# An ordering edge behind each score's relu for the projection work between the indexer's scores of row blocks 2 and 3

## The chip, the cores and the metric

The kernel runs on one core of a Trainium2 chip. The metric is the device time of one execution in microseconds (us). Engines are named as in the profile: PE (matrix products, with PEld for its weight loads), ACT, DVE, POOL, and SP, which here only issues DMAs. Every engine works through its own queue in order; engines wait for each other through semaphores. A line number L374 is a line of the kernel before; in the kernel after, lines from 365 on stand one or two further down.

## The reference

One transformer block over 512 positions of width 1024, in float32. Branch A is sparse attention: an indexer scores all pairs, each row keeps its best 128 keys, and a softmax with a relative bias runs over those. Branch B is stick-breaking attention. Gates, an output projection, a layer norm and a gated MLP with a causal convolution follow.

```python
proj = x @ w_in[layer]
q_a, k_a, v_a, q_i, k_i, w_i, q_s, k_s, v_s, g_a, g_b = jnp.split(proj, IN_OFFSETS, axis=-1)
...
dots = jnp.einsum('thd,sd->ths', qib, k_idx).astype(jnp.float32) * IDX_DIM ** -0.5
score = jnp.einsum('th,ths->ts', wib.astype(jnp.float32), jax.nn.relu(dots))
score = jnp.where(key_chunk[None, :] <= q_chunk, score, -jnp.inf)
_, sel = lax.top_k(score, n_sel)
...
log_beta = jax.nn.log_sigmoid(z)
log_keep = jnp.where(causal, jax.nn.log_sigmoid(-z), 0.0)
later = lax.cumsum(log_keep, axis=2, reverse=True) - log_keep
a = jnp.where(causal, jnp.exp(log_beta + later), 0.0).astype(v.dtype)
```

## The kernel before

Every float32 operand is split into a high part and the remainder (names ending in h and l, or whi and wlo for weights), and a product is made of three matmuls: high by high, high by low, low by high. A weight piece is loaded by SP, its high part is made by ACT (L101) and its low part by DVE or, for the projections in POOL_LO (qs, ks, gb, qa0, ka0, va), by POOL (L103). The pieces run through rings of three buffers, three loads and three splits ahead of use (`Stream`), so a split waits for the last matmul on the piece three before it.

**The projections are fillers.** FILL lists them in order: the rest of the value projection vs, then query, key and gate projections (qs0, ks0, ..., gb, qa, ka, va). `fill(n)` issues the next n matmuls of that list, and at a projection's end its evictions: the copy on ACT (L252 for values, L326 for queries, L315 and L316 for keys), the remainder on DVE (L253, L327, L317, L318), for queries also a DMA from ACT's queue (L328). The fillers fill the gaps of the attention work: three matmuls after each score, GAP = 15 at three points of each head.

**The scores.** `idx_scores` (L365) runs over row blocks j = 1, 2, 3 and eight heads: two matmuls into a bank of pool psA (`dot_ps`, L371, L372; 256, 384, 512 columns for the three blocks), a relu on ACT into an SBUF tile (L374), and a multiply-add on DVE into score j (L377, L379). psA has four banks, shared with the projections of the fillers. At each step of the loop (L580) one selection round is issued for j > 1, and then `fill(3)`.

**Selection.** `select` finds the best 128 of each row in 16 rounds of MAX and MATCH_REPLACE on DVE (L388, L389) and ends with a TENSOR_SCALAR (L391). The rounds left over are spread over the heads by ROUNDS.

**Heads.** Eight stick-breaking heads, then eight sparse ones. For each the next head's logits are issued first (z_ps, L452, with two sigmoids on ACT, L456 and L457), then the weights of this one are transposed (tr_ps, L410; evicted to pth on ACT, L414, and ptl on DVE, L415), then the next head's running products are made by four scans on DVE (L466) and a product on POOL (beta, L468), then the value product (av_ps, L426, with avt on ACT, L431, and yst on DVE, L432). A sparse head has logits l_ps (L490) with a reduction (L494) on DVE, an exponential on ACT (L496) and a scaling on DVE (L502), and a mask bm on POOL (L479).

**What sets the order.** The code's order is not the final one: a scheduler reorders the instructions of every engine by a simulated timeline, within the dependencies. `tc.issue_after(x)` adds one: whatever is issued inside it stays behind instruction x in the order. The kernel uses it at L602 to L605 for scans and selection.

## Time and profile before

| | us |
|---|---|
| median of 3 runs | 762.83 (762.15 to 762.95) |
| profiled execution, its own time | 762.16 |
| its span, first to last instruction | 760.4 |
| PE busy | 748.6 |
| DVE busy | 555.4 |
| ACT busy | 379.3 |
| POOL busy | 153.5 |
| granted clock of TensorE | 0.998 |

The page gives the busy time of each engine, the chain of work that ended last, and the costliest groups. The waits view lists, for each engine, the instruction that waited, what released it, the total, the count and the longest. The timeline lists instructions of one engine by start and duration; like neighbours are drawn together with a count, and square brackets give the idle time before an instruction and what ended it. In the timeline the durations of PE overlap, since matmuls are pipelined; what a matmul costs is the distance between starts.

The scores run from about 49 to 66 us, the heads follow, then the output projection and the MLP. The stretches that matter below are the scores and the heads from 150 to 212 us, which include the end of the stick-breaking heads and the first sparse ones.

### The profile page before, as it was taken

How to read it: one execution, taken by the hardware profiler on the slowest of the kernel's cores; microseconds unless marked ns; L12 is line 12 of the kernel's file. 1: busy time of each engine (PE TensorE's matmuls, PEld its weight loads, DVE VectorE, ACT ScalarE, POOL GpSimd, SP SyncE). 2: the span in 40 equal slices, each digit the busy share in tenths (PEclk: the TensorE clock that was granted, in tenths of full speed). 3: DMA queues.
4: the chain of work that ended last, by engine and by line, in shares of the span. 5: the costliest groups of instructions: out<-in, count | busy, mean ns of one | idle time of the engine just before them, and what ended most of it. 6: DMA issues, size and time to landing. Idle time of an engine off the chain costs nothing.

```text
span 760.4 us, 9842 instructions
## 1 busy us (share of the span) xinstructions
PE 748.6 (98%) x3573; PEld 627.3 (82%) x3573; DVE 555.4 (73%) x905; ACT 379.3 (50%) x568; POOL 153.5 (20%) x160
## 2 busy tenths in 40 slices
PE   9999999999999999999999999999999999999995
PEld 7878888887888888888889888888888888888885
DVE  5569787799878585548765867766776768668995
ACT  5474756655574756835364633433443344346430
POOL 1002555426644210000111110111011101110012
PEclk9999999999999999999999999999999999999999
DMA  8445433232223324116942344544444444448632
GB/s 267 147 128 181 125 95 96 72 111 84 80 102 111 111 76 122 64 60 206 340 61 84 139 156 136 155 137 139 153 140 142 147 138 137 141 152 274 222 105 79
DMA packets 40448, 102.89 MB, mean 135 GB/s; under 512 B 10888, under 2 KB 11272, under 8 KB 40400
## 3 DMA queue, kind: packets, MB, share of 16 engines
q1 hardware_dynamic: 34672, 85.98, 35.4%
q0 software_dynamic: 3728, 11.04, 4.0%
q10 hardware_dynamic: 2000, 5.24, 2.8%
q8 instruction: 28, 0.46, 0.3%
q14 instruction: 20, 0.16, 0.1%
HBM read 88.59 MB, written 9.98 MB: 130 GB/s over the span
## 4 chain that ended last, share of the span: by engine, by line
PE 92%; DVE 5%; issue 1%; ACT 0%; POOL 0%; POOLq 0%; ACTq 0%; DVEq 0%
PE u_ps L774 5%; PE u_ps L776 5%; PE g_ps L774 5%; PE u_ps L775 5%; PE g_ps L776 5%; PE g_ps L775 5%; PE m L856 2%; PE m L854 2%; PE m L855 2%; PE av_ps L426 2%; PE ga_ps L224 2%; PE ga_ps L223 2%; PE ga_ps L225 2%; PE o_ps L704 2%; PE o_ps L703 2%; PE o_ps L705 2%
## 5 line engine op out<-in xcount | busy, mean ns | idle before, releaser
L101 ACT ACTIVATE whi<-raw 128x1024 fp32r<-128x1024 f32 (+1 forms) x124 | 124.1, 1001 | 169.5 <-PE g_ps L775 44.9
L103 DVE TENSOR_TENSOR wlo<-raw,whi 128x1024 fp32r<-128x1024 f32 (+1 forms) x105 | 120.0, 1144 | 41.3 <-ACT whi L101 40.5
L776 PE MATMUL u_ps<-x1h,wlo 128*128 128x512 f32 (+1 forms) x192 | 71.4, 372 | 0.0
L774 PE MATMUL u_ps<-x1h,whi 128*128 128x512 f32 (+1 forms) x192 | 71.3, 372 | 0.0
L775 PE MATMUL u_ps<-x1l,whi 128*128 128x512 f32 (+1 forms) x192 | 71.3, 371 | 0.0
L774 PE MATMUL g_ps<-x1h,whi 128*128 128x512 f32 (+1 forms) x184 | 69.9, 380 | 0.0
L775 PE MATMUL g_ps<-x1l,whi 128*128 128x512 f32 (+1 forms) x184 | 69.9, 380 | 0.0
L776 PE MATMUL g_ps<-x1h,wlo 128*128 128x512 f32 (+1 forms) x184 | 69.9, 380 | 0.0
L103 POOL TENSOR_TENSOR wlo<-raw,whi 128x1024 fp32r<-128x1024 f32 x19 | 45.8, 2412 | 34.5 <-ACT whi L101 34.4
L776 PEld LDWEIGHTS u_ps<-x1h,wlo 128*128 128x128 f32 x192 | 36.2, 188 | 6.3
L775 PEld LDWEIGHTS u_ps<-x1l,whi 128*128 128x128 f32 x192 | 36.2, 188 | 6.3
L774 PEld LDWEIGHTS u_ps<-x1h,whi 128*128 128x128 f32 x192 | 36.2, 188 | 6.2
L415 DVE TENSOR_TENSOR ptl<-tr_ps,pth 128x512 fp32r<-128x512 f32 (+1 forms) x48 | 27.9, 595 | 18.2 <-ACT pth L414 17.6
L776 PEld LDWEIGHTS g_ps<-x1h,wlo 128*128 128x128 f32 x184 | 34.6, 188 | 6.6
L775 PEld LDWEIGHTS g_ps<-x1l,whi 128*128 128x128 f32 x184 | 34.6, 188 | 6.5
L774 PEld LDWEIGHTS g_ps<-x1h,whi 128*128 128x128 f32 x184 | 34.6, 188 | 6.5
L797 DVE TENSOR_TENSOR t<-raw 128x512 f32<-128x512 f32 x11 | 7.6, 693 | 40.2 <-DMA raw<-in_w_fo_dram 40.2
L816 POOL MEMSET u<- 128x2 f32 x22 | 2.1, 98 | 143.7 <-ACT whi L101 99.9
L830 DVE TENSOR_TENSOR hF<-g_ps,c 128x512 f32<-128x512 f32 x22 | 15.1, 687 | 20.4 <-PE g_ps L776 20.4
L822 ACT ACTIVATE c<-c,cwt 128x512 f32<-128x512 f32 x22 | 16.0, 725 | 26.3 <-DVE c L821 26.1
L672 POOL TENSOR_TENSOR rstd<-rstd,mhalf 128x1 f32<-128x1 f32 x8 | 7.6, 951 | 106.0 <-DVE rstd L671 106.0
L414 ACT ACTIVATE pth<-tr_ps 128x512 fp32r<-128x512 f32 (+1 forms) x48 | 23.9, 520 | 9.8 <-PE tr_ps L410 6.8
(566 smaller groups left out, 2055.9 us busy)
## 6 DMA issues: line engine op xcount, KB each, us to landing
raw<-in_w_fi_dram SPq DMA_DIRECT2D x44, 512.0 KB, 3.3
raw<-in_w_t_dram SPq DMA_DIRECT2D x32, 512.0 KB, 3.4
raw<-in_w_fo_dram SPq DMA_DIRECT2D x26, 512.0 KB, 4.2
raw<-in_w_br_dram SPq DMA_DIRECT2D x8, 512.0 KB, 3.3
raw<-in_w_o_dram SPq DMA_DIRECT2D x8, 512.0 KB, 4.2
raw<-in_w_v_dram SPq DMA_DIRECT2D x7, 512.0 KB, 3.9
raw_b<-in_w_fo_dram SPq DMA_DIRECT2D x6, 512.0 KB, 4.2
s_t<-t POOLq DMA_DIRECT2D x11, 256.0 KB, 2.3
```

What stands on the lines that cost most here:

```text
L101: nc.scalar.activation(hi[:, :w], t[:, :w], AF.Copy)
L103: self.done[key] = eng.tensor_sub(lo[:, :w], t[:, :w], r32(hi[:, :w])).ins
L223: nc.tensor.matmul(ps[:M], wh[:, c], xh[k], start=(k == 0), stop=False)
L224: nc.tensor.matmul(ps[:M], wh[:, c], xl[k], start=False, stop=False)
L225: nc.tensor.matmul(ps[:M], wl[:, c], xh[k], start=False, stop=(k == KC - 1))
L414: nc.scalar.activation(th[:, :width], ps[:, :width], AF.Copy)
L415: lows = nc.vector.tensor_sub(tl[:, :width], ps[:, :width], r32(th[:, :width]))
L426: nc.tensor.matmul(ps[:, 128 * i:512], vt[i][:, h].rearrange("p a d -> p (a d)"), t[i], start=(n == 0), stop=(n == len(seq) - 1))
L774: nc.tensor.matmul(ps[:, c], wh[:, kc], x1h[:, k, c], start=(k == 0), stop=False)
L775: nc.tensor.matmul(ps[:, c], wh[:, kc], x1l[:, k, c], start=False, stop=False)
L776: nc.tensor.matmul(ps[:, c], wl[:, kc], x1h[:, k, c], start=False, stop=(k == KC - 1))
L822: nc.scalar.activation(c, c, AF.Gelu_apprx_tanh, bias=cwt[:, f, 3:4])
```

## The change

`idx_scores` hands out, with j, the relu instruction of the score before. For the steps of j > 1, that is from block 2's first score on, the loop issues `fill(3)` inside `issue_after` of that relu: whatever a filler issues there on ScalarE, split or eviction, is ordered behind the last score's relu. No computation is added or taken away, and no operand changes.

```diff
--- before.py
+++ after.py
@@ -362,16 +362,17 @@
 
     def idx_scores():
         kih, kil, wi = index["k"]
+        last = None
         for j in (1, 2, 3):
             N = 128 * (j + 1)
             for h in range(H):
-                yield j
+                yield j, last
                 ps = pa("dot_ps")
                 r = slice(j * 128, j * 128 + 128)
                 nc.tensor.matmul(ps[:, :N], qi[h][:, r], kih[:, :N], start=True, stop=False)
                 nc.tensor.matmul(ps[:, :N], qi[h][:, r], kil[:, :N], start=False, stop=True)
                 rl = bp.tile([128, 512], F32, tag="pt", bufs=8, name="relu")
-                nc.scalar.activation(rl[:, :N], ps[:, :N], AF.Relu, scale=0.125)
+                last = nc.scalar.activation(rl[:, :N], ps[:, :N], AF.Relu, scale=0.125).ins
                 w = wi[:, j - 1, h:h + 1]
                 if h == 0:
                     nc.vector.tensor_scalar(score[j], rl[:, :N], w, None, op0=ALU.mult)
@@ -577,10 +578,11 @@
     nc.gpsimd.dma_start(s_win, bass.AP(tensor=s_line.tensor, offset=s_line.offset + 127,
                                        ap=[[NREL, H], [-1, 128], [1, 512]]))
 
-    for j in idx_scores():
+    for j, last in idx_scores():
         if j > 1:
             select_some(1)
-        fill(3)
+        with tc.issue_after(last) if j > 1 else nullcontext():
+            fill(3)
     heads = [("s", h) for h in range(H)] + [("a", h) for h in range(H)]
 
     def start_head(i):
```

The edge changes the scheduler's timeline, so it also moves rows far behind the scores, through the heads. Three places follow. At the first, ACT in the middle of the scores, relu_478 to relu_547 are block 1's, those with 384 columns block 2's; vs0 to vs3 are the evictions of the value projection, whi_16 is a split for a weight piece. Before:

```order
L374 ACTIVATE relu_478<-dot_ps_475 128x256
L252 ACTIVATE vs0_704<-vs_ps0_163 128x8x64
L252 ACTIVATE vs1_707<-vs_ps1_164 128x8x64
L374 ACTIVATE relu_487<-dot_ps_484 128x256
L252 ACTIVATE vs2_710<-vs_ps2_165 128x8x64
L374 ACTIVATE relu_496<-dot_ps_493 128x256
L374 ACTIVATE relu_505<-dot_ps_502 128x256
L101 ACTIVATE whi_16_604<-raw_16_602 128x1024
L252 ACTIVATE vs3_713<-vs_ps3_166 128x8x64
L374 ACTIVATE relu_520<-dot_ps_517 128x256
L374 ACTIVATE relu_529<-dot_ps_526 128x256
```

After, from the fourth relu of block 1 on:

```order
L375 ACTIVATE relu_505<-dot_ps_502 128x256
L375 ACTIVATE relu_520<-dot_ps_517 128x256
L375 ACTIVATE relu_529<-dot_ps_526 128x256
L375 ACTIVATE relu_538<-dot_ps_535 128x256
L375 ACTIVATE relu_547<-dot_ps_544 128x256
L375 ACTIVATE relu_560<-dot_ps_557 128x384
L375 ACTIVATE relu_572<-dot_ps_569 128x384
L375 ACTIVATE relu_584<-dot_ps_581 128x384
L375 ACTIVATE relu_596<-dot_ps_593 128x384
L101 ACTIVATE whi_16_604<-raw_16_602 128x1024
L375 ACTIVATE relu_614<-dot_ps_611 128x384
L375 ACTIVATE relu_626<-dot_ps_623 128x384
```

whi_16 moved from between block 1's fourth and fifth relu to between block 2's fourth and fifth; vs0 to vs3 moved behind block 3's fourth relu, eight rows further down.

The second place is in the stick-breaking heads, near 155 to 166 us. On DVE, keep_1505 is the last of four scans of one head, m8 and MATCH_REPLACE are selection rounds of blocks 2 and 3, wlo_30 is the low part of a weight piece, ka0a and ka0b are key evictions, yst2 belongs to a value product. Before:

```order
L388 MAX m8_1578<-score2_369 128x8
L388 MAX m8_1583<-score3_370 128x8
L327 SCALAR_TENSOR_TENSOR qa0b_1627<-qa0_ps_1541,qa0b_1627 64x512
L389 MATCH_REPLACE score2_369<-m8_1578,score2_369 128x384
L389 MATCH_REPLACE score3_370<-m8_1583,score3_370 128x512
L391 TENSOR_SCALAR score2_369<-score2_369 128x384
L388 MAX m8_1586<-score3_370 128x8
L432 TENSOR_TENSOR yst2_1610<-av_ps_1611,avt_1620 64x512
L389 MATCH_REPLACE score3_370<-m8_1586,score3_370 128x512
L103 TENSOR_TENSOR wlo_30_1637<-raw_30_1634,whi_30_1636 128x1024
L388 MAX m8_1589<-score3_370 128x8
L317 TENSOR_TENSOR ka0a_1685<-ka0_ps_1640,ka0a_1685 64x512
```

After:

```order
L467 SCALAR_TENSOR_TENSOR keep_1505<-keep_1505,first_96 128x256
L389 MAX m8_1578<-score2_369 128x8
L389 MAX m8_1583<-score3_370 128x8
L103 TENSOR_TENSOR wlo_30_1637<-raw_30_1634,whi_30_1636 128x1024
L317 TENSOR_TENSOR ka0a_1685<-ka0_ps_1640,ka0a_1685 64x512
L318 TENSOR_TENSOR ka0b_1686<-ka0_ps_1640,ka0b_1686 64x512
L390 MATCH_REPLACE score2_369<-m8_1578,score2_369 128x384
L390 MATCH_REPLACE score3_370<-m8_1583,score3_370 128x512
L433 TENSOR_TENSOR yst2_1610<-av_ps_1611,avt_1620 64x512
L392 TENSOR_SCALAR score2_369<-score2_369 128x384
L389 MAX m8_1586<-score3_370 128x8
```

wlo_30 and the two key evictions moved from behind the second selection round to directly behind the scans and two MAX; qa0b's row moved ahead of the scans; the TENSOR_SCALAR that ends block 2's selection stands behind them and behind yst2. The next DVE row of the following head, ptl_1707, has the same rows ahead of it as before, in another order.

On PE at the same place, gb4 is a gate projection, qa1 the query projection behind it, and tr_ps are the ten transposes of a head. Before:

```order
L223 MATMUL gb4_ps_1697<-xh6_324,whi_28_1484 128x512
L224 MATMUL gb4_ps_1697<-xl6_325,whi_28_1484 128x512
L410 MATMUL tr_ps_1701<-ident_91,beta_1504 128x128 x4
L410 MATMUL tr_ps_1710<-ident_91,beta_1504 128x128 x4
L410 MATMUL tr_ps_1719<-ident_91,beta_1504 128x128 x2
L225 MATMUL gb4_ps_1697<-xh6_324,wlo_28_1485 128x512
L223 MATMUL gb4_ps_1697<-xh7_346,whi_28_1484 128x512
L224 MATMUL gb4_ps_1697<-xl7_347,whi_28_1484 128x512
L225 MATMUL gb4_ps_1697<-xh7_346,wlo_28_1485 128x512
```

After:

```order
L225 MATMUL gb4_ps_1697<-xh7_346,wlo_28_1485 128x512
L223 MATMUL qa1_ps_1794<-xh0_131,whi_29_1537 128x512
L224 MATMUL qa1_ps_1794<-xl0_132,whi_29_1537 128x512
L225 MATMUL qa1_ps_1794<-xh0_131,wlo_29_1538 128x512
L223 MATMUL qa1_ps_1794<-xh1_185,whi_29_1537 128x512
L224 MATMUL qa1_ps_1794<-xl1_186,whi_29_1537 128x512
L411 MATMUL tr_ps_1701<-ident_91,beta_1504 128x128 x4
L225 MATMUL qa1_ps_1794<-xh1_185,wlo_29_1538 128x512
L223 MATMUL qa1_ps_1794<-xh2_227,whi_29_1537 128x512
L224 MATMUL qa1_ps_1794<-xl2_228,whi_29_1537 128x512
L225 MATMUL qa1_ps_1794<-xh2_227,wlo_29_1538 128x512
L411 MATMUL tr_ps_1710<-ident_91,beta_1504 128x128 x4
```

The ten transposes moved from ahead of gb4's last four matmuls to behind the fifth matmul of qa1 and later. The same holds for the other heads: the transposes that begin with tr_1548 stand behind 15 matmuls of qa0 before, and behind all 24 of qa0 and 13 of ka0 after; those of the last stick-breaking head but one stood ahead of va's first matmul and are now among its first. Later, gb5's first matmuls stood behind six transposes and two logit products, and now stand ahead of them. The value eviction on DVE for which gb5 waits (L253, va0) now stands ahead of two reductions (L494) and of yst3.

The third place is ACT a little later, near 171 to 183 us; keep_1805 and beta_1804 are the sigmoids of a head's logits, avt_1773 is a value product's copy, qa1a and qa1b are the two halves of a query eviction, each with a DMA that waits for DVE's half. Before:

```order
L431 ACTIVATE avt_1773<-av_ps_1764 64x512
L456 ACTIVATE keep_1805<-z_ps_1812 128x512
L457 ACTIVATE beta_1804<-z_ps_1812 128x512
L456 ACTIVATE keep_1805<-z_ps_1819 128x256
L457 ACTIVATE beta_1804<-z_ps_1819 128x256
L101 ACTIVATE whi_32_1790<-raw_32_1788 128x1024
L326 ACTIVATE qa1a_1887<-qa1_ps_1794 64x512
L437 ACTIVATE ys2h_1776<-yst2_1610 128x512
L328 DMA qa1a_1887<-qa1a_1887 64x1024
L414 ACTIVATE pth_1844<-tr_ps_1839 128x512
L326 ACTIVATE qa1b_1888<-qa1_ps_1794 64x512
```

After:

```order
L326 ACTIVATE qa1a_1887<-qa1_ps_1794 64x512
L457 ACTIVATE keep_1805<-z_ps_1807 128x512
L458 ACTIVATE beta_1804<-z_ps_1807 128x512
L328 DMA qa1a_1887<-qa1a_1887 64x1024
L432 ACTIVATE avt_1773<-av_ps_1764 64x512
L457 ACTIVATE keep_1805<-z_ps_1812 128x512
L458 ACTIVATE beta_1804<-z_ps_1812 128x512
L457 ACTIVATE keep_1805<-z_ps_1819 128x256
L458 ACTIVATE beta_1804<-z_ps_1819 128x256
L326 ACTIVATE qa1b_1888<-qa1_ps_1794 64x512
L438 ACTIVATE ys2h_1776<-yst2_1610 128x512
L328 DMA qa1b_1888<-qa1b_1888 64x1024
```

The DMA of qa1a moved from behind avt_1773, the sigmoids and ys2h to ahead of them. On DVE, qa1b's row moved two selection rounds, a MAX and ptl_1845 further ahead, and ka1a and ka1b moved ahead of ptl_1845 and the scans of keep_1805. On POOL the splits L103 of the fillers moved ahead of the beta products (L468) of the heads; on SP one weight load, raw_19, stands behind two loads of win; in the last layer norm, the low split b22_0l stands one row of L677 later on DVE.

## The prediction, made before the result was known

> **What bounds the kernel now.** I read the page's first and fourth parts, then the waits of PE, then tables by stretch, and only then single instructions.
>
> ```profile
> PE 748.6 (98%) x3573; PEld 627.3 (82%) x3573; DVE 555.4 (73%) x905; ACT 379.3 (50%) x568; POOL 153.5 (20%) x160
> ...
> PE 92%; DVE 5%; issue 1%; ACT 0%; POOL 0%; POOLq 0%; ACTq 0%; DVEq 0%
> ```
>
> PE is busy 98% of the span and makes 92% of the chain that ended last. ACT, on which the change acts, is busy half the time and makes none of that chain. The change removes no matmul, so it can gain only where PE waits:
>
> ```profile
> PE dot_ps L371 <- ACT relu L374: 1.0, 1, 1.0
> PE va_ps L244 <- DVE ka1b L318: 0.9, 1, 0.9
> PE gb_ps L223 <- DVE va L253: 0.5, 1, 0.5
> ```
>
> The columns are the total, the count and the longest. Beside the kernel's start, which is not touched, these three are all there is to gain: 2.4 us, and some 0.2 us more for each, since the start after a wait comes late by more than the wait that is counted (below). So the change can hardly give more than 3 us, 0.4%. What it can lose has no such bound, because from 150 us on PE runs only just ahead of a full VectorE:
>
> ```profile
> 160.00:170.00 10.00, 10.00 (x51) 8.39 (x50) 9.86 (x19) 4.73 (x9) 2.40 (x1) 1.00 0.27 79
> 200.00:210.00 10.00, 10.00 (x53) 8.13 (x52) 7.05 (x19) 5.39 (x13) 7.67 (x8) 1.00 0.44 129
> ```
>
> The columns are length, PE, PEld, DVE, ACT, POOL, granted clock, DMA share, GB/s. DVE works 9.86 of 10 us at 160 to 170; only at 200 to 210 has it 2.95 us to spare. The clock is 1.00 throughout.
>
> **Part 1: the scores, 50 to 66 us.** This is the place that the words of the change name.
>
> ```profile
> 51.75 1.06 ACT L101 ACTIVATE whi<-raw 128x1024 fp32r<-128x1024 f32 x1
> ...
> 53.19 5.67 ACT L374 ACTIVATE relu<-dot_ps 128x256 f32<-128x256 f32 x14
> ...
> 52.33 0.28 PE L372 MATMUL dot_ps<-kil,qi3b 128*128 128x256 f32 x1
> 53.62 0.44 PE L371 MATMUL dot_ps<-kih,qi0a 128*128 128x384 f32 x1 [1.01 <-ACT relu L374]
> ...
> 56.36 0.34 PE L372 MATMUL dot_ps<-kil,qi3b 128*128 128x384 f32 x1
> ...
> 58.45 0.43 PE L223 MATMUL qs_ps<-xh,whi 128*128 128x512 f32 x1
> ```
>
> Four psA banks take turns, so block 2's first dot product waits for the relu of block 1's fifth, which in ACT's queue stands behind whi_16 (1.06 us) and vs3. The two starts lie 1.29 us apart where 0.12 us is the pitch of such matmuls: **1.17 us** lost, against 1.01 counted as idle. In the new ACT order that relu stands directly behind the one before it, so this wait goes.
>
> What is late next: whi_16 now stands inside block 2, ahead of its fifth relu, whose bank block 3's first dot needs. A pair of dots is issued every 0.37 us (53.62 to 56.36 holds 15 starts), a relu takes 0.405 us (5.67 over 14), so over eight scores ACT falls back 0.3 us, and with whi_16 1.3 us. Four banks give four pairs, 1.5 us, of which dot and relu themselves use some 0.8; the remaining 0.7 doesn't cover 1.3. I estimate a wait of 0.6 to 0.7 at block 3's first dot. Net **-0.5 us**, between -1.17 (the slack covers it) and 0 (the wait only moves). The four vs evictions now stand behind block 3's fourth relu, and their banks are next asked for by head s0's transposes, behind ks0, qs1, ks1 and qs2, 96 matmuls. Their VectorE halves go with them; up to 188 us PE waits for nothing on DVE, so I cost that at nothing. SP's raw_19 now stands behind two window loads; the weights run a ring of three ahead, so nothing too.
>
> **Part 2: 150 to 212 us, where VectorE has no cover.** The scheduler reorders everything behind the edge: transposes and the value product of each stick-breaking head stand 12 to 22 projection matmuls later in PE's order, and some evictions change place on DVE.
>
> ```profile
> 146.75 0.60 PE L410 MATMUL tr_ps<-ident,beta 128*128 128x128 f32 x4
> ...
> 162.57 1.25 PE L410 MATMUL tr_ps<-ident,beta 128*128 128x128 f32 x10
> 163.58 0.47 PE L225 MATMUL gb_ps<-xh,wlo 128*128 128x512 f32 x1
> ...
> 164.37 0.39 PE L225 MATMUL gb_ps<-xh,wlo 128*128 128x512 f32 x1
> ...
> 179.24 0.40 PE L244 MATMUL va_ps<-whi,xh 128*128 128x512 f32 x1
> 179.47 0.39 PE L245 MATMUL va_ps<-wlo,xh 128*128 128x512 f32 x1
> ...
> 210.55 0.50 PE L223 MATMUL gb_ps<-xh,whi 128*128 128x512 f32 x1 [0.53 <-DVE va L253]
> ```
> ```profile
> 148.02 0.69 DVE L415 TENSOR_TENSOR ptl<-tr_ps,pth 128x512 fp32r<-128x512 f32 x1
> ...
> 153.16 2.95 DVE L466 TENSOR_TENSOR_SCAN keep<-keep,first 128x128 f32<-128x128 f32 x4
> 156.04 1.12 DVE L388 MAX8 m<-score 128x8 f32<-128x384 f32 x2
> 157.19 0.69 DVE L327 SCALAR_TENSOR_TENSOR qa0b<-qa_ps,qa0b 64x512 fp32r<-64x512 f32 x1
> ...
> 159.15 0.35 DVE L391 TENSOR_SCALAR score<-score 128x384 f32<-128x384 f32 x1
> ...
> 161.41 1.21 DVE L103 TENSOR_TENSOR wlo<-raw,whi 128x1024 fp32r<-128x1024 f32 x1
> ...
> 165.46 0.69 DVE L415 TENSOR_TENSOR ptl<-tr_ps,pth 128x512 fp32r<-128x512 f32 x1
> ```
> ```profile
> 156.19 2.45 POOL L468 TENSOR_TENSOR beta<-beta,keep 128x1280 f32<-128x1280 f32 x1 [8.23 <-DVE keep L466]
> ...
> 165.75 2.40 POOL L103 TENSOR_TENSOR wlo<-raw,whi 128x1024 fp32r<-128x1024 f32 x1 [6.95 <-ACT whi L101]
> ```
>
> First, what happens when POOL reads SBUF under certain DVE operations:
>
> ```profile
> 182.31 2.40 POOL L103 TENSOR_TENSOR wlo<-raw,whi 128x1024 fp32r<-128x1024 f32 x1 [3.16 <-ACT whi L101]
> ...
> 198.61 2.42 POOL L103 TENSOR_TENSOR wlo<-raw,whi 128x1024 fp32r<-128x1024 f32 x1 [2.94 <-ACT whi L101]
> ```
> ```profile
> 183.56 3.97 DVE L466 TENSOR_TENSOR_SCAN keep<-keep,first 128x128 f32<-128x128 f32 x4
> ...
> 200.24 1.08 DVE L391 TENSOR_SCALAR score<-score 128x512 f32<-128x512 f32 x1
> ```
>
> The four scans take 2.95 us at 153.16, with POOL idle, and 3.97 at 183.56, inside POOL's 182.31 to 184.71. The TENSOR_SCALAR of L391 takes 0.35 us on 384 columns at 159.15, with POOL idle, but 1.08 on 512 at 200.24, while POOL runs until 201.03. So these operations stand still until POOL's instruction ends. [...]
>
> Now the walk along DVE's new order. The block of ten transposes (tr_1548 first) stands 22 matmuls later, each 0.227 us (179.24 to 179.47): 146.75 + 5.0 - 0.5 = 151.25. From tr_ps to ptl it is 1.27 us (146.75 to 148.02): ptl_1554 at 152.5; three ptl and qa0b, 2.35 us, then the scans 154.85 to 157.8 (before: 153.16 to 156.1). POOL's beta product follows the scans, 157.85 to 160.3. Two MAX (1.15) and DVE asks for wlo_30 at 158.95, which like the scans reads two tiles in SBUF: by the scans' example it stands until 160.3 (before, wlo at 161.41 met an idle POOL). Then wlo_30 1.2, ka0a and ka0b 1.4, two MATCH 1.25 (157.9 to 159.15), yst2 0.65 (64x512, as qa0b): the TENSOR_SCALAR asks at 164.8.
>
> POOL's next split, wlo_31, follows the end of gb4. That comes earlier now, since the ten transposes (162.57 to 163.58) stand behind gb4's last matmul: 164.37 + 0.23 - 1.0 - 0.5 = 163.1, and with whi (165.75 - 164.6 = 1.15) POOL runs **164.25 to 166.65**. So L391 waits 1.85 us. A round of selection is
>
> ```profile
> L388 DVE MAX8 m<-score 128x8 f32<-128x512 f32 x16 | 11.0, 685 | 0.2
> L389 DVE MATCH_REPLACE8 score<-m,score 128x512 f32<-128x512 f32 x16 | 10.8, 676 | 0.0
> ```
>
> 1.45 us with its value load; L391 and two rounds put ptl_1707 at 169.85 against 165.46: **DVE is 4.4 us late** with the same work done. What PE then waits for:
>
> ```profile
> 181.24 0.69 DVE L327 SCALAR_TENSOR_TENSOR qa1b<-qa_ps,qa1b 64x512 fp32r<-64x512 f32 x1
> ...
> 209.80 1.29 DVE L253 TENSOR_TENSOR va<-va_ps,va 128x512 fp32r<-128x512 f32 x2 [1.21 <-ACT va L252]
> ```
>
> *qa1b.* It now stands two rounds (2.9), a MAX and a ptl (1.4) further ahead: 181.24 + 4.4 - 4.3 = 181.35, ended 182.0. Its bank is taken by va_ps2. Ten transposes that stood ahead of va's first matmul (179.24) are now behind it: 179.24 - 1.0 - 0.5 = 177.75, then transposes 1.0 and six matmuls 1.36: PE asks at 180.1 and waits **1.9 us**. The old wait for ka1b (0.9) goes, since ka1b now stands ahead of the scans.
>
> *va0, on which gb5 waits.* Of the 4.4 us the collisions at 183.56 and 200.24 give back 1.0 and 0.6, because PE and POOL have passed; between none and all of the 2.95 us idle at 200 to 210 comes off too; and va0 now stands ahead of two reductions and yst3, 1.4 us. So its eviction starts at 208.2 to 211.2, I take 209.7, and frees the bank 0.75 later. gb5 started at 210.55 with 1.9 us of waits behind it, so 208.6 without them; it now stands ahead of six transposes and two logit products, an estimated 1.0 us, and 0.5 are gained at the scores: PE asks at 207.1 + 1.9 = 209.0, a wait of **1.5 us**, with bounds 0 and 3.
>
> Together 3.4 us, where before these two places lost 0.9 + 0.5 and some 0.2 each on the restart, 1.8 to 1.9. Term: **+1.6**, bounds -1.8 (both waits gone) and +4.
>
> **Part 3: small terms.** Transposes cost PE the same 0.1 us each in a run of four or ten (162.57 to 163.58); only where runs are cut differently is there something to lose: +0.1, bounds 0 and 0.3. In the tail
>
> ```profile
> 735.37 1.22 DVE L103 TENSOR_TENSOR b_0l<-raw_b,b_0h 128x1024 fp32r<-128x1024 f32 x1
> 736.50 1.41 DVE L677 SCALAR_TENSOR_TENSOR r<-r,rstd,ln 128x512 f32<-128x512 f32 x2
> ...
> 737.14 0.40 PE L855 MATMUL m<-b_0l,bh 128*128 128x512 f32 x1
> ```
>
> the split at 735.37 stands one L677 (0.66) later, so it ends at 737.25, after PE asks: +0.1, bounds 0 and 0.1.
>
> **Sum:** -0.5 + 1.6 + 0.1 + 0.1 = +1.3 on the profiled execution's own 762.16 us: 763.46. That execution lay 0.67 below the median of the runs shown (762.83) and with the lowest of them; I add half of that: **763.8 us**.
>
> **Rivals.**
> - *L391 slips in ahead of POOL's wlo_31* (its margin is 164.8 - 164.25 = 0.55 us). For it: 0.55 is little after 100 us of walk. Against it: wlo_30's block at 158.95 is wide. Then DVE is 2.55 late, qa1b ends at 180.2 and va2 hardly waits, gb5 about 0.9: -0.5 - 0.9 + 0.2 = -1.2, so **761.3**.
> - *Slower: ACT blocks behind its own DMA.* In the new order ACT issues the DMA of qa1a ahead of avt_1773 and four sigmoids; the DMA waits for DVE's qa1a (175.5 + 1.45 + 0.7 = 177.65). ACT's half of qa1b then ends at 180.85, 0.5 before DVE asks. If DVE is over 0.5 later still, each engine waits for the other in turn and va2's wait grows 1 to 2 us: **765 to 766**. For it: the two queues now interlock at three points. Against it: 0.5 us of slack.
> - *Waits only move:* the score wait reappears whole at block 3 and DVE gets back its lag before gb5: 0, **762.5**. Here the change does nothing to the path although it moves rows.
>
> **Chances.** Forecast 45% (own range 762.9 to 764.9), L391 first 25%, ACT blocked 20%, waits only move 10%. A measurement of this kernel can tell about 0.2%, 1.5 us, from no change: faster means under 761.3, slower over 764.4. The forecast gives same 32, slower 13; L391 first gives faster 16, same 9; ACT blocked slower 20; the last same 8, faster 2. So 0.18, 0.49, 0.33. The range runs from half a microsecond under the fast rival to the end of the slow one, 760.8 to 766.0; outside are the far bounds of the terms.
>
> **What would show it.** In PE's waits the line for L371 falls from 1.0 to 0.6 or 0.7 and stands at block 3. On DVE the L391 on 384 columns takes about 2.1 us instead of 0.35, with POOL's wlo under it; the scans near 186 take 2.95 instead of 3.97. PE's waits show qa1b (or yst2 ahead of it) near 180 for about 1.9, and va at gb5 for about 1.5. The forecast is wrong if L391 is not stretched, if the score stage still waits a full microsecond, or if PE waits before 150 us for something that waited for nothing before.

## The result, and the profile after

| | before | after |
|---|---|---|
| median us (lowest to highest), 6 runs each | 762.49 (761.68 to 763.48) | 768.88 (768.18 to 770.54) |
| after over before, 95% interval | | 1.0088 (1.0078 to 1.0097) |
| profiled execution, its own time, us | 762.16 | 769.45 |
| its span, us | 760.4 | 767.7 |

The change makes the kernel 6.4 us slower, 0.9%. The prediction, 763.8 us, had the direction but a fifth of the size, and its range ended at 766.0.

The first line is from the page of after, the busy times.

```profile
PE 752.5 (98%) x3573; PEld 628.9 (82%) x3573; DVE 571.1 (74%) x905; ACT 379.4 (49%) x568; POOL 154.9 (20%) x160
```

The instructions that compute are the same, 905 on DVE, yet DVE is busy 15.7 us longer: some of them take longer than before. Now PE's waits in after, with the total, the count and the longest:

```profile
PE tr_ps L411 <- DVE mn L495: 3.2, 1, 3.2
...
PE tr_ps L411 <- DVE yst L433: 0.7, 1, 0.7
PE dot_ps L372 <- ACT relu L375: 0.6, 1, 0.6
...
PE av_ps L427 <- DVE ptl L416: 0.3, 1, 0.3
PE ks_ps L223 <- ACT relu L375: 0.2, 1, 0.2
PE va_ps L244 <- DVE qa1b L327: 0.2, 1, 0.2
```

The old waits for ka1b and for va (gb5) are gone. The relu wait fell from 1.0 to 0.6, as forecast, but has a companion at ks0. The large one is new: transposes that wait for DVE. These are its rows on PE, and then the two stretches around it in the table by stretch (PE, PEld, DVE, ACT, POOL, granted clock, DMA share, GB/s):

```profile
209.98 0.39 PE L246 MATMUL va_ps<-whi,xl 128*128 128x512 f32 x1
213.53 1.11 PE L411 MATMUL tr_ps<-ident,lg 128*128 128x128 f32 x4 [3.16 <-DVE mn L495]
...
216.15 0.63 PE L224 MATMUL gb_ps<-xl,whi 128*128 128x512 f32 x1
216.57 0.63 PE L225 MATMUL gb_ps<-xh,wlo 128*128 128x512 f32 x1
```
```profile
200.00:210.00 10.00, 10.00 (x51) 8.29 (x49) 8.50 (x19) 3.97 (x9) 6.26 (x6) 1.00 0.42 133
210.00:220.00 10.00, 6.84 (x23) 5.49 (x22) 9.18 (x18) 5.93 (x14) 3.31 (x5) 0.66 0.29 85
```

PE stands for 3.16 us, and when it goes on, its 512-column matmuls start 0.42 us apart (216.15 to 216.57) instead of 0.227: the granted clock is 0.66 in the mean of that stretch. It had been 1.00 in before.

The wait is put down to mn, the accumulator of a reduction, though what the transposes read is lg, which the scalings L503 write. The scalings stand just ahead of that reduction in DVE's queue. DVE and POOL there, in after:

```profile
204.79 0.42 DVE L392 TENSOR_SCALAR score<-score 128x512 f32<-128x512 f32 x1
206.60 0.69 DVE L495 CUSTOM_DVE_ANT_0 lg<-l_ps,bm 128x512 f32<-128x512 f32 x1 [1.40 <-POOL bm L480]
...
207.22 1.69 DVE L103 TENSOR_TENSOR wlo<-raw,whi 128x1024 fp32r<-128x1024 f32 x1
...
209.36 3.50 DVE L503 TENSOR_SCALAR lg<-lg,rs 128x128 f32<-128x128 f32 x4
212.79 0.68 DVE L495 CUSTOM_DVE_ANT_0 lg<-l_ps,bm 128x512 f32<-128x512 f32 x1
213.40 0.08 DVE L495 DVE_READ_ACCUMULATOR2_ANT mn<- 128x1 f32 x1
```
```profile
205.28 2.54 POOL L480 TENSOR_TENSOR bm<-win,score 128x512 f32<-128x512 f32 x2 [2.24 <-DVE score L392]
...
209.47 3.11 POOL L480 TENSOR_TENSOR bm<-win,score 128x256 f32<-128x256 f32 x3
```

And the same rows in before:

```profile
203.96 0.69 DVE L494 CUSTOM_DVE_ANT_0 lg<-l_ps,bm 128x512 f32<-128x512 f32 x1 [0.54 <-POOL bm L479]
...
204.78 1.28 DVE L502 TENSOR_SCALAR lg<-lg,rs 128x128 f32<-128x128 f32 x4
205.97 1.22 DVE L103 TENSOR_TENSOR wlo<-raw,whi 128x1024 fp32r<-128x1024 f32 x1
```
```profile
206.23 3.77 POOL L479 TENSOR_TENSOR bm<-win,score 128x256 f32<-128x256 f32 x3
```

In before the four scalings took 1.28 us and ended at 206.06, and POOL's mask adds for a later head began at 206.23: they missed each other by 0.17 us. In after the split wlo_36 stands ahead of the scalings; they start at 209.36, the mask adds at 209.47, and the four take 3.50 us. The selection that all of this follows ended at 201.32 in before (1.08 from 200.24) and at 205.21 in after (0.42 from 204.79): 3.9 us late.

Why PE goes on behind mn and not behind the scalings: the transposes also need a bank. tr_ps, l_ps, av_ps and z_ps share the four banks of pool psB. Between 204.05 and 209.69 in after PE wrote into all four: one took a value product (av_ps), three took the next head's logits (l_ps). DVE copies the value product out only at 216.50, so the first bank to come free is that of the logits which the reduction at 212.79 reads. In before that reduction stood ahead of the scalings (203.96); now it stands behind them. So the scalings hold PE up twice: of the 3.16 us, the first 2.5 pass until lg is there (212.86), and some 0.7 more until the bank is free (213.48, PE at 213.53). In late_after, wlo36_later, pool_before and edge_j3, which are told below, PE begins these transposes 0.05 to 0.06 us behind that reduction too.

To see where time goes in every version alike, I added up, over all matmuls of a trace, the distance from each start to the next less the pitch of its width in before (0.227, 0.173, 0.119 and 0.061 us for 512, 384, 256 and 128 columns, as read in unbroken runs of projections, scores and value products). It holds what PE loses to waits and to a low clock, and also what a transpose (0.109 us behind another in before) takes beyond 0.061. In us by stretch, for these two kernels and for the experiments that are told below:

| us | before | after | late_ after | late_ before | wlo36_ later | edge_ j3 | pool_ before | scale_ after |
|---|---|---|---|---|---|---|---|---|
| to 40 | 2.6 | 2.9 | 2.8 | 3.6 | 3.4 | 3.1 | 2.3 | 2.1 |
| 40 to 70 | 2.1 | 2.4 | 2.1 | 2.4 | 2.5 | 1.5 | 2.5 | 2.4 |
| 70 to 170 | 5.0 | 4.8 | 5.0 | 4.8 | 4.8 | 5.0 | 4.8 | 4.8 |
| 170 to 205 | 3.2 | 4.3 | 2.9 | 8.7 | 4.3 | 4.5 | 3.7 | 4.3 |
| 205 to 220 | 1.7 | 6.5 | 1.9 | 1.7 | 1.6 | 4.4 | 5.0 | 1.8 |
| 220 to 345 | 5.5 | 6.2 | 8.5 | 5.7 | 9.8 | 8.6 | 5.8 | 5.9 |
| 345 to end | 0.1 | 0.3 | 0.3 | 0.1 | 0.3 | 0.7 | 0.3 | 0.3 |
| sum | 20.1 | 27.3 | 23.4 | 27.0 | 26.7 | 27.8 | 24.4 | 21.6 |

pe_before is not in the table: the one of its five executions that has a trace took 1265.94 us, at a granted clock of 0.557.

The sum of after is 7.3 above that of before, as are the spans (767.7 - 760.4). Of these, 0.3 lie in the first 40 us, which the change doesn't touch and which vary by 1.5 us among these traces; 0.3 at the scores, 1.1 at 170 to 205, **4.8 at 205 to 220**, and 0.9 behind.

### The profile page after: what moved, and what is told of

It reads as the page before. It is cut to its first block, busy times and chain, and to the rows that moved or that the text cites. A ratio compares the mean times of both kernels' runs of the same rounds, so it can differ in the third digit from the quotient of the medians.

```text
span 767.7 us, 9848 instructions
## 1 busy us (share of the span) xinstructions
PE 752.5 (98%) x3573; PEld 628.9 (82%) x3573; DVE 571.1 (74%) x905; ACT 379.4 (49%) x568; POOL 154.9 (20%) x160
## 4 chain that ended last, share of the span: by engine, by line
PE 89%; DVE 8%; issue 1%; DMA 1%; ACT 1%; POOL 0%; POOLq 0%; SPq 0%; ACTq 0%; DVEq 0%
PE u_ps L778 5%; PE u_ps L776 5%; PE g_ps L778 5%; PE u_ps L777 5%; PE g_ps L776 5%; PE g_ps L777 5%; PE m L857 2%; PE m L858 2%; PE m L856 2%; PE av_ps L427 2%; PE ga_ps L224 2%; PE ga_ps L225 2%; PE ga_ps L223 2%; PE o_ps L705 2%; PE o_ps L707 2%; PE o_ps L706 2%
## 5 line engine op out<-in xcount | busy, mean ns | idle before, releaser
L103 DVE TENSOR_TENSOR wlo<-raw,whi 128x1024 fp32r<-128x1024 f32 (+1 forms) x105 | 121.9, 1162 | 43.3 <-ACT whi L101 42.8
L103 POOL TENSOR_TENSOR wlo<-raw,whi 128x1024 fp32r<-128x1024 f32 x19 | 48.9, 2576 | 26.4 <-ACT whi L101 26.4
L467 DVE TENSOR_TENSOR_SCAN keep<-keep,first 128x128 f32<-128x128 f32 (+3 forms) x32 | 34.2, 1126 | 0.0
```

The costliest lines, as they stand in the source:

```text
L103: self.done[key] = eng.tensor_sub(lo[:, :w], t[:, :w], r32(hi[:, :w])).ins
L467: scan = nc.vector.tensor_tensor_scan(rev, rev, first[:, 512 - N:512][:, ::-1], 0.0, op0=ALU.mult, op1=ALU.max)
```

## The experiments

The theory after the first look: the score stage is innocent; the order that the scheduler chose behind it makes DVE late at the end of the selection, and at the sparse heads DVE then runs into POOL's mask adds. The rivals: the score stage itself is dearer than it looks; POOL's weight splits under the scans, seen in the trace, are the whole lateness; one badly placed split (wlo_36) is the whole loss; the half clock is the loss.

To change the order of one place without the rest, most kernels hold the scheduler to a given order. A helper adds an order-only edge from each instruction of an engine to the next one of a table:

```diff
+def pin(tc, table):
+    traced = {}
+    for i in tc.nc.cur_bb.bb.instructions:
+        traced.setdefault(str(i.engine).split(".")[-1], []).append(i)
+    for engine, runs in table.items():
+        order = [traced[engine][a + k] for a, n in runs for k in range(n)]
+        for first, then in zip(order, order[1:]):
+            tc.add_manual_dep(then, first.name, mybir.DependencyInfo(mybir.DependencyClass.NoSync, mybir.DependencyReason.DATA), reason="pin")
...
         tile_block(tc, *args)
+        pin(tc, PINS)
```

Where an experiment below says "pinned", this is its edit, and what its table holds is said in words. Times are medians, ratios are against before in the same batch (its medians there: 762.48 to 762.67).

### Which part of the order loses the time

**scores_after**: the edge of the change, with PE, DVE, ACT and POOL pinned to the order of before from the end of the scores on.

> The changed kernel with its new order kept at the scores (up to about 66 us), and every engine's order behind them held to that of the kernel before. Theory R (nearly all of the loss comes from the rows that moved behind the scores: scans that now run under POOL's weight splits make DVE 4 to 6 us late, PE feels it at 180 and above all at 210 us): within 1 us of the kernel before, 762 to 763.5; no wait of PE over 1.2 us behind the scores. Rival S (the edge itself, at the scores, costs the time): 767 to 769.5. My prediction's own term for the scores alone would give -0.5 us, about 762.0; the trace after shows +0.3 there, about 762.8.

**scores_before**: no edge; everything behind the scores pinned to the order of after.

> The other half: the kernel before with its own order at the scores, and behind them every engine held to the order of the changed kernel, without the edge. Theory R: 768 to 769.5, with five groups of scans stretched by about 2 us each and a wait of PE near 210 us of over 2 us. Rival S: 762 to 763.5.

Measured: 762.73 us, 1.0004 (0.9995 to 1.0012), and 768.28 us, 1.0083 (1.0069 to 1.0096). The whole loss comes with the order behind the scores, and none that these runs can tell with the scores. In scores_after the old wait of 1.0 at block 2 is replaced by 0.6 and 0.2, and that is no gain.

**edge_j2** and **edge_j3**: the edge for one of the two row blocks only, nothing pinned.

```diff
-        with tc.issue_after(last) if j > 1 else nullcontext():
+        with tc.issue_after(last) if j == 2 else nullcontext():
```

(`j == 3` in edge_j3.)

> The changed kernel with the edge for the second row block alone. The order behind the scores is then nearly that of the kernel before (some 60 PE rows of 3200 in another place, 690 against the changed kernel). Theory R (the order behind the scores makes the loss, whichever edge triggers it): 761.5 to 763.5. Rival (each edge costs its share, as a cost of holding ScalarE back): half of the loss, about 765.

> The changed kernel with the edge for the third row block alone. PE's order at the scores is that of the kernel before, the order behind them nearly that of the changed kernel (5 PE rows differ). Theory R: 767.5 to 769.5. Rival (each edge costs its share): about 765.

Measured: 763.65 us, 1.0016 (1.0007 to 1.0025), just above the expected 763.5, and 768.33 us, 1.0077 (1.0063 to 1.0091). With the edge for block 2 alone the order behind the scores stays nearly that of before; with block 3's alone it turns into nearly that of after, and the time with it. So the eight edges of block 3 tip the scheduler's simulated timeline into another order through all the heads. Block 2's edge still costs 1.2 us, most of it at the scores: there edge_j2 loses 3.0 us by the measure of the table, where before loses 2.1, with waits of 0.64 at block 3's first dot and 0.75 at ks0.

**late_before** and **late_after**: the two orders joined near 205 us, at a set of instructions that both have done by then. late_before is after until there, and then pinned to the order of before; late_after is the reverse.

> The changed kernel up to about 205 us, and from there (selection's end, first sparse head) every engine held to the order of the kernel before. Theory D (DVE arrives 4 to 6 us late at 205 us, and PE must wait for that lateness somewhere between 205 and 250 us whatever the local order): 766 to 769, with waits of 3 us or more in all behind 205. Theory L (the local order behind 205 us, wlo_36 and the scalings under POOL's mask adds, makes the loss): 763 to 765.

> The mirror: the kernel before up to about 205 us, then the order of the changed kernel. Theory D: DVE is on time, so the late order costs little: 762 to 764, the wait at the first transposes under 1 us. Theory L: 765.5 to 768, with a wait over 2 us there.

Measured: 769.25 us, 1.0089 (1.0073 to 1.0104), and 765.59 us, 1.0039 (1.0026 to 1.0051). The late order alone costs 3.1 us. The first look at late_after's waits, DVE and POOL:

```profile
PE av_ps L426 <- DVE ptl L415: 2.1, 2, 1.3
...
205.06 3.55 DVE L502 TENSOR_SCALAR lg<-lg,rs 128x128 f32<-128x128 f32 x4
...
205.13 3.19 POOL L479 TENSOR_TENSOR bm<-win,score 128x256 f32<-128x256 f32 x3
```

DVE is not late there (the selection ends at 200.9), and still the scalings run under the mask adds, as in after. Here PE doesn't stand at the transposes but later, for ptl, near 236 and 249 us. In late_before the scalings of the first four heads take 1.27, 2.38, 2.67 and 5.51 us, as in before (1.28, 2.39, 2.66, 5.51), and the table shows no loss behind 205. But PE waited 3.28 us at the joint, a wait that neither kernel has:

```profile
203.34 0.46 PE L411 MATMUL tr_ps<-ident,beta 128*128 128x128 f32 x2 [3.28 <-DVE mn L495]
```

These transposes read beta, which has nothing to do with mn: this too is a wait for a bank that logits hold until their reduction. So this run can't price the early order by itself; that it makes DVE late, and that PE pays for it somewhere, is what it shows.

### What makes DVE late, and what its lateness costs

**pool_before**: after, with POOL pinned to the order of before and the other engines to that of after.

> The changed kernel, only POOL held to the order of the kernel before behind the scores: the beta product of a head stands ahead of the next weight split, so a split can't start while the scans run. Theory R, in its port form (POOL's splits stop the scans): the scans of all heads go back to about 2.95 us a group, DVE busy falls by 7 to 9 us, ptl_1707 is 0 to 2 us late instead of 5.7, the wait at 210 us falls under 1.5 us; 763 to 765. Rival: DVE's lag comes from its own order (transposes that stand later), and not from POOL: then the lag stays over 4 us and the time over 767. Second rival: splits that wait for beta come too late for PE, which then waits for wlo on POOL: over 766 with new waits of PE on L103.

Measured: 767.98 us, 1.0067 (1.0055 to 1.008); the expected 763 to 765 was missed. (That a port is what stops the scans, no run shows; the runs show the durations.) The group of scans in after, and in pool_before (total busy us, mean ns):

```profile
L467 DVE TENSOR_TENSOR_SCAN keep<-keep,first 128x128 f32<-128x128 f32 (+3 forms) x32 | 34.2, 1126 | 0.0
```
```profile
L467 DVE TENSOR_TENSOR_SCAN keep<-keep,first 128x128 f32<-128x128 f32 (+3 forms) x32 | 23.9, 804 | 0.0
```

The ten us that the scans lost in after are gone, and only about 1 us of time comes back (768.88 to 767.98). Most of what the scans lose to POOL is absorbed earlier, where DVE had time to spare: at the next scans pool_before is 2.65 us ahead of after (155.42 against 158.07). Another collision then takes back 1.5 of these. L392, free of POOL in after (0.34 us at 168.02), stands in pool_before under POOL's split of 164.57 to 166.95:

```profile
165.38 1.80 DVE L392 TENSOR_SCALAR score<-score 128x384 f32<-128x384 f32 x1
```

So DVE reaches ptl_1707 at 170.00 instead of 171.19 and is still 4.5 us behind before's 165.46.

**short_after** and **short_before**: four of block 3's sixteen selection rounds work on 16 columns instead of 512, in the order of after and of before (all pinned). Part of the selection is left out in both, and DVE has less to do before 205 us.

```diff
-        for _ in range(NSEL // 8):
+        for n in range(NSEL // 8):
...
-            nc.vector.max(m8, sc)
-            nc.vector.match_replace(sc, m8, sc, TAKEN)
+            part = sc[:, :16] if j == 3 and 4 <= n < 8 else sc
+            nc.vector.max(m8, part)
+            nc.vector.match_replace(part, m8, part, TAKEN)
```

> The changed kernel with every engine held to its own order; four of the sixteen selection rounds of row block 3 (DVE, 177 to 184 us in the trace after) work on 16 columns instead of 512, so that part of the computation is left out. That gives DVE back about 5 us just before the place where PE begins to wait; nothing else is changed. Theory D (what PE loses is DVE's lateness): 762 to 764, the wait at the sparse head's first transposes under 0.7 us, no waits on ptl later. Theory L (the late order by itself): 765.5 to 768, a wait over 2 us stays. Control beside it: the kernel before with the same rounds shortened.

> The control: the kernel before, held to its own order, with the same four rounds on 16 columns (the same part of the computation left out). Its waits for ka1b (0.9) and va (0.5) should go, nothing else: 760.5 to 762 by either theory. What the changed kernel loses beyond this one is then not DVE's lateness at 184 us.

Measured: 766.75 us, 1.0052 (1.0038 to 1.0066), and 760.59 us, 0.9971 (0.9959 to 0.9983). Both gain some 2 us, and the difference stays at 6.2. In short_after the scalings still take 3.52 us. A few us of DVE's time ahead of the place don't take the collision away: POOL's mask adds follow DVE's selection, so both come earlier together (scalings at 208.08, mask adds at 208.20, each 1.3 earlier than in after).

**pe_before**: after, with PE alone pinned to the order of before, to learn whose order makes the early lateness.

> The changed kernel with PE alone held to the order of the kernel before behind the scores; DVE, ACT and POOL keep the changed order. Open is what made DVE late by 205 us. Theory T (PE's order: transposes 12 to 22 matmuls later): DVE's lateness at ptl_1707 falls from 5.7 to under 3 us. Theory Q (the queue order on DVE itself: split and evictions ahead of selection): it stays over 4 us, and PE, whose transposes now ask earlier than DVE's order serves them, waits more: 768 to 772.

Measured: 776.78 us (all but the one with the trace between 775.14 and 778.74), 1.0183 (1.0167 to 1.0199), beyond what was expected. The rows of its one trace can't be set against the others. A PE order taken out of its own DVE order is worse than either; which engine's order makes DVE late before 205 us stays open.

### What at 205 to 220 us takes the time

**wlo36_later**: after, with one DVE row moved (pinned).

```diff
-L103 TENSOR_TENSOR wlo_2089<-raw_2086,whi_2088 128x1024
 L416 TENSOR_TENSOR ptl<-tr_ps,pth 128x256
 L500 RECIPROCAL rs<-sm 128x4
...
 L253 TENSOR_TENSOR va_2207<-va_ps_1945,va_2207 128x8x64
+L103 TENSOR_TENSOR wlo_2089<-raw_2086,whi_2088 128x1024
```

> The changed kernel with one DVE row moved: the split wlo_36 stands behind the four scalings, the next head's first reduction and va0 instead of ahead of the scalings. Theory L (the local order at 207 us decides: the split costs 1.7 us and lets POOL's mask adds catch the scalings, 3.5 us instead of 1.3): scalings 1.3 to 2 us, PE's wait of 3.2 us at the first transposes falls under 1 us, TensorE's clock stays 1.0 there, 763.5 to 765.5. Rival (lateness alone: the selection ended 3.9 us late, and the order only moves the wait): the wait falls by less than 1 us and the time stays at 767.5 to 769.

Measured: 768.75 us, 1.0081 (1.0068 to 1.0093): nothing gained. The first head's scalings take 1.27 us again, the wait at 210 us and the low clock are gone, and the table shows 1.6 at 205 to 220. But its waits for ptl have grown from 0.3 us to 3.3, 3.1 of them behind 220, where the three other heads' scalings take 3.51, 4.67 and 5.14 us:

```profile
PE av_ps L427 <- DVE ptl L416: 3.3, 4, 1.7
```

The loss moved to 220 to 345 (9.8). So neither the one row nor the half clock is the loss: DVE is behind, and PE meets it a head later. edge_j3 says the same of the clock. A stretch of after, then the same of edge_j3:

```profile
214.00:216.00 2.00, 2.00 (x8) 1.71 (x7) 1.45 (x7) 1.98 (x7) 0.00 (x0) 0.50 0.31 57
```
```profile
214.00:216.00 2.00, 2.00 (x10) 1.69 (x11) 1.44 (x6) 1.98 (x6) 0.00 (x0) 1.00 0.41 117
```

edge_j3 has the same wait (3.1 us) and keeps the full clock; it then waits 2.1 us for ptl behind 220, and its time is that of after. After loses 6.5 us at 205 to 220 and 6.2 behind, edge_j3 4.4 and 8.6: in after, where the clock dropped, PE was held back and had less to wait for later.

**scale_after** and **scale_before**: the scalings of the first four sparse heads go to ACT, in the order of after and of before (pinned but for those rows).

```diff
-            nc.vector.tensor_scalar(lg[:, c], lg[:, c], rs[:, j:j + 1], None, op0=ALU.mult)
+            if h < 4:
+                nc.scalar.activation(lg[:, c], lg[:, c], AF.Copy, scale=rs[:, j:j + 1])
+            else:
+                nc.vector.tensor_scalar(lg[:, c], lg[:, c], rs[:, j:j + 1], None, op0=ALU.mult)
```

> The changed kernel, held to its own order, with the four scalings (L503) of the first four sparse heads on ACT instead of DVE; same results. [...] Theory P (the late order puts DVE's scalings under POOL's mask adds, 3.5 to 5 us a head instead of 1.3 to 2.7, and this is what PE waits for at 210 and again near 238 and 252 us): the wait at 210 falls from 3.2 to under 1.2, the waits on ptl stay away, TensorE's clock stays at 1.0, 764 to 766. Theory D (DVE is late anyway and the waits only move): 767 to 769.

> The control: the kernel before, held to its own order, with the same scalings on ACT. PE waits nowhere for them there, so by theory P and D alike 761.5 to 763.0; if ACT's queue gets in the way (exponentials behind scalings that wait for DVE's reciprocal), up to 764.

Measured: 764.69 us, 1.0027 (1.0017 to 1.0037), and 765.89 us, 1.0037 (1.0023 to 1.0052). In the order of after it gives back 4.2 of the 6.4 us. The first head's scalings on ACT in scale_after, and the line that is left of the large wait:

```profile
208.58 1.93 ACT L504 ACTIVATE lg<-lg,rs 128x128 f32<-128x128 f32 x4 [0.72 <-DVE rs L500]
...
PE tr_ps L411 <- ACT lg L504: 0.3, 1, 0.3
```

They take 1.93 us while POOL's mask adds run, and the table shows 1.8 and 5.9 behind 205, against 1.7 and 5.5 in before: nearly the whole loss behind 205 is gone, and most of the rest is that of 170 to 205 and of the scores. The control says that this is no general gain. In the order of before the same move costs some 3 us (762.58 to 765.89, with runs from 763.80 to 767.84), beyond the expected 764, because ACT's queue then holds up other work. The waits of scale_before, in a trace of its slowest execution, in which the clock was also at 0.50 from 213 to 219 us:

```profile
PE gb_ps L223 <- DVE va L253: 1.5, 1, 1.5
PE l_ps L490 <- DVE mn L494: 1.2, 1, 1.2
```

One limit: the move takes the scalings' own time off DVE as well as what they lose to POOL, 14.7 us together in after (3.50, 3.48, 2.54 and 5.15). So it shows that the scalings in DVE's queue are what holds PE up, by their own result and by the reduction behind them. How much of that is what they lose to POOL is read from the durations alone, 3.50 against 1.28; no run moves POOL's mask adds and nothing else.

### A version that beats both

**best1**: before, with only whi_16 and vs3 moved behind block 3's fourth relu on ACT, and their halves on DVE (pinned). **best2**: best1, with ka1a and ka1b ahead of the scans on DVE, and the copy of va0 on ACT directly ahead of ys3h.

```diff
 L415 TENSOR_TENSOR ptl<-tr_ps,pth 128x256
+L317 TENSOR_TENSOR ka1a<-ka_ps,ka1a 64x512
+L318 TENSOR_TENSOR ka1b<-ka_ps,ka1b 64x512
 L466 SCALAR_TENSOR_TENSOR keep<-keep,first 128x128
...
+L252 ACTIVATE va_2207<-va_ps_1945 128x8x64
 L437 ACTIVATE ys3h<-yst_1917 128x512
 L496 ACTIVATE lg,sm<-lg,mn 128x256
-L252 ACTIVATE va_2207<-va_ps_1945 128x8x64
```

> A version that has the change's aim without its side: the kernel before, held to its own order, with only two ACT rows moved: whi_16 and vs3 stand behind block 3's fourth relu (their DVE halves follow). The wait of 1.0 us at block 2's first dot goes; block 3's first dot has its bank in time, since ACT paces no further behind. Expected 761.2 to 762.0; by the rival (the wait moves to block 3 or to ks0, as in the changed kernel) 762.3 to 762.9.

> best1, and the two waits on DVE as well: ka1a and ka1b stand ahead of the scans they stood behind, and ACT's copy of va0 ahead of ys3h and one exponential. If all three waits go without a new one: 759.3 to 760.5. Rival (DVE is full from 150 to 205 us, so the waits only move): 761 to 762.5.

Measured: 761.68 us, 0.9985 (0.9976 to 0.9994), and 759.93 us, 0.9961 (0.9947 to 0.9975). best1 has no relu wait left; best2 has none of the three that the prediction called all there is to gain. Its only line of PE's waits, and the scans that stood under POOL in before (3.97 us at 183.56):

```profile
PE idle_ps L200 <- DVE idle L197: 1.2, 1, 1.2
...
184.38 2.97 DVE L466 TENSOR_TENSOR_SCAN keep<-keep,first 128x128 f32<-128x128 f32 x4
```

The gain of 2.7 us is close to the bound of 3 that the prediction read from PE's waits.

## Why the prediction was right and wrong

**What bounds the kernel: right.** The gain was bounded by 3 us (best2 got 2.7), and the loss was not; it came from the stretch where PE runs just ahead of a full DVE.

**Part 1, the scores, -0.5: wrong in sign.** The wait at block 2 went, and block 3's first dot waits 0.62, losing 0.78, in the range forecast. But ACT stays behind to the stage's end: ks0 loses another 0.39 and block 3's last score 0.19, behind the rows that had moved there and that the prediction did not follow so far. The old loss of 1.17 became 1.36 and restarts, 0.3 more in the table; scores_after, with 1.0004, shows no gain.

**Part 2, DVE's walk, 4.4 us late at ptl_1707: near in number, in part by luck.**

```profile
161.99 2.65 DVE L103 TENSOR_TENSOR wlo<-raw,whi 128x1024 fp32r<-128x1024 f32 x1
...
168.02 0.34 DVE L392 TENSOR_SCALAR score<-score 128x384 f32<-128x384 f32 x1
...
171.19 0.68 DVE L416 TENSOR_TENSOR ptl<-tr_ps,pth 128x512 fp32r<-128x512 f32 x1
```
```profile
161.11 2.46 POOL L469 TENSOR_TENSOR beta<-beta,keep 128x1280 f32<-128x1280 f32 x1 [8.91 <-DVE keep L467]
...
165.10 2.40 POOL L103 TENSOR_TENSOR wlo<-raw,whi 128x1024 fp32r<-128x1024 f32 x1 [1.38 <-ACT whi L101]
```

It was 5.7 us (171.19 - 165.46). wlo_30 stood behind POOL's beta as forecast, 2.65 us instead of 1.21. L391's block did not come: it ran at 168.02, half a us behind the end of POOL's split at 167.50, in 0.34 us. In its place the walk began too early: the scans that it put at 154.85 began at 158.07, 3.2 us later, and 4.4 + 3.2 - 1.85 is about the 5.7. Most of that arose before 150 us, where the walk had not looked: five groups of scans stand under POOL's splits. One of them in after, on DVE and on POOL:

```profile
99.65 4.66 DVE L467 TENSOR_TENSOR_SCAN keep<-keep,first 128x128 f32<-128x128 f32 x4
...
99.08 2.40 POOL L103 TENSOR_TENSOR wlo<-raw,whi 128x1024 fp32r<-128x1024 f32 x1 [3.90 <-ACT whi L101]
```

The text ahead of the forecast notes that the splits moved ahead of the beta products on POOL; the walk gave it no price. pool_before tells what that left out: with POOL's old order both named blocks come (wlo_30 2.66 us, L392 1.80), and ptl_1707 stands at 170.00, where the walk had 169.85. In time it is about 1 us.

**qa1b and yst2 near 180, 1.9 us: right in place, smaller.** PE loses 0.91 for yst2 and 0.37 for qa1b, 1.3, and 0.75 more at two value products that wait for ptl; the ka1b wait (1.1 with its restart) went. The stretch gives +1.1 where the forecast's terms give +0.8 (1.9 less 0.9 and 0.2).

**"va0, on which gb5 waits", 1.5 us: the step that failed.** PE never got as far as that wait. Six transposes that stood ahead of gb5 in before stand behind its first matmuls in after, as the prediction said, but the first four still stand ahead of gb5, and on these PE stood for 3.16 us. The walk carried DVE from ptl_1707 to va0 by counting rows moved, with the durations of before; it had no row for the scalings, though it named the kind, a TENSOR_SCALAR that stands still until POOL's instruction ends. They were free of POOL in before by 0.17 us; in after they took 2.2 us more. Nor did it ask what those four transposes wait for besides: their bank, held until a reduction that had moved behind the scalings. So the stretch 205 to 220 cost 4.8 us more than before, instead of 0.8 (1.5 less 0.5 and 0.2). The step failed, and not only its size: the wait stood at other matmuls, for other rows of DVE, and these had been put at nothing.

**The rivals.** "ACT blocks behind its own DMA" did happen, at two heads. ACT in after:

```profile
154.54 0.47 ACTq L328 DMA_DIRECT2D qa0a<-qa0a  x1
155.05 0.60 ACT L415 ACTIVATE pth<-tr_ps 128x512 fp32r<-128x512 f32 x1 [2.80 <-DVE qa0a L327]
...
173.65 0.59 ACT L458 ACTIVATE beta<-z_ps 128x512 f32<-128x512 f32 x1
178.92 0.47 ACTq L328 DMA_DIRECT2D qa1a<-qa1a  x1
...
181.71 0.59 ACT L326 ACTIVATE qa1b<-qa_ps 64x512 fp32r<-64x512 f32 x1
```

At the place that the prediction named, it issued nothing from 174.24, when its sigmoid ended, to 178.92, when the DMA of qa1a went out. That made nobody late: ACT's half of qa1b ended at 182.30 and DVE took it up at 182.55, a margin of 0.25 us. At the head before it did cost. The transposes began at 152.32, but the copy pth stands behind qa0a's DMA, which waited for DVE's half of qa0a (153.82 to 154.50), and DVE then stood for that copy:

```profile
155.68 0.69 DVE L416 TENSOR_TENSOR ptl<-tr_ps,pth 128x512 fp32r<-128x512 f32 x1 [1.18 <-ACT pth L415]
```

So part of the 3.2 us by which the scans came later than the walk had them is this interlock: a DVE that is late makes ACT late, and that makes DVE wait. "L391 ahead of wlo_31" and "waits only move" did not happen.

**Standing still under POOL.** The prediction read it from a group of scans and one TENSOR_SCALAR of before; after shows it again. wlo_30 at 161.99 ended at 164.64, 1.07 us behind the end of POOL's beta at 163.57. Stopped whole, it would have had all its 1.21 us left then; at half rate for the 1.58 us before, only 0.42. So it stood still for nearly all of that time.

## What to carry to other kernels

Where a scheduler orders the work, an order-only edge on work that nobody waits for can still change everything behind it: before and after such an edit, compare the order far from the edit, or pin it, and then change one place. Where instructions of one engine take longer while another's run (here four scalings on DVE, 1.28 us ahead of POOL's mask adds and 3.50 under them), look in the trace for pairs that only just miss each other (here by 0.17 us) and that both follow the same event; here a shift of one row (1.27 us in wlo36_later), not a change of load (3.52 in short_after), decided whether they collide. When a removed wait gives nothing, add up what PE loses over the whole stretch: here, from 170 to 345 us, it was 10.3 us in before and 13.3 to 17.5 in every version with after's late order and the scalings on DVE, wherever the waits stood.

## What the runs showed of the hardware

By the traces' record of the granted clock it stood at 0.50 for 6.8 us, from 212.19 on, around the idle time of 3.16 us in after, and for 3.4 us, from 212.95 on, around one of only 2.14 us in pool_before; around one of 3.15 us in edge_j3 it did not fall. In after it fell while PE still stood, 1.8 us after its last matmul. In pool_before it fell some 1.6 us after PE had begun again, and the distance between matmul starts goes from 0.23 to 0.43 us:

```profile
211.34 0.66 PE L411 MATMUL tr_ps<-ident,lg 128*128 128x128 f32 x4 [2.14 <-DVE mn L495]
...
212.74 0.44 PE L223 MATMUL gb_ps<-xh,whi 128*128 128x512 f32 x1
212.97 0.63 PE L224 MATMUL gb_ps<-xl,whi 128*128 128x512 f32 x1
213.40 0.63 PE L225 MATMUL gb_ps<-xh,wlo 128*128 128x512 f32 x1
```

So in these three traces the length of the idle time alone doesn't decide whether the clock falls; what does, no run shows.
